# Reordering a two-lane decoder kernel: next sequence's FFN moved up, the convolution cut in three, one projection by tiles, two more buffers

## The chip, the cores and the metric

One Trainium2 chip, eight cores in two dies (cores 0 to 3 and 4 to 7). Each core computes two of the sixteen sequences, and no core waits for another. The metric is the device time in microseconds of the slowest core. The runs of this program show a fast state and a slow one: in the slow one the cores of one die (sometimes of both) record a lower granted TensorE clock, and the time is longer. For the kernel before, fast runs took from 6699 us and slow ones up to 7793. Wherever I compare kernels below, I use one of two things: the *fast runs* (no die over 1% longer than the other at a lower clock, and no run over 1.5% above the fastest of its kernel), or the *undisturbed dies*, by which I mean the dies of any run whose clock (the median of its four cores) is within 0.003 of the best of that kernel on that chip, each by its slowest core. The second gives more samples, because also in a slow run one die is usually undisturbed (of after's nine slow runs, in eight). It has no confidence interval here; I give its number of samples.

## The reference

A decoder of two layers, model width 1024, 2048 positions, FFN width 2816. Per layer:

```python
x = x + 0.5 * swiglu_ffn(rms_norm(x, ffn1_norm[l]), ffn1_w_up[l], ffn1_w_down[l])
h = rms_norm(x, mix_norm[l])                     # one projection h @ w_in, split over four groups
o_a = hgrn2_mixer(...)                           # gated recurrence, chunkwise
o_b = gla_mixer(...)                             # gated linear attention, chunkwise
o_c = dilated_attention_mixer(...)               # three dilated windows, partial rotary
o_d = conformer_conv_mixer(...)                  # GLU -> causal depthwise conv 31 -> LayerNorm -> swish
x = x + jnp.concatenate([o_a, o_b, o_c, o_d], axis=-1) @ w_out[l]
x = x + memory_cross_attention(rms_norm(x, cross_norm[l]), rms_norm(mem, mem_norm[l]), ...)
x = x + 0.5 * swiglu_ffn(rms_norm(x, ffn2_norm[l]), ffn2_w_up[l], ffn2_w_down[l])
# after the layers: rms_norm(x, final_norm)
```

The four groups o_a to o_d read the same `h` and are independent of each other until they are added into `x` through `w_out`. The change uses that freedom, and the freedom between two sequences.

## The kernel before

The kernel is written as a program that *records* operations. Every operation belongs to one of two lanes: **F** (the FFNs, with PSUM banks 0 to 3 and the weight buffers WBF and WS) and **M** (mixer and cross attention, with banks 4 to 7 and the sixteen buffers MU). A list scheduler then fixes the order on each engine: for each engine and lane it looks at the next 40 operations in program order, and takes the one that can start first by its own estimates. So the two lanes mix freely, but a lane can't look far beyond its own place in the program. All operations are issued from one line, which is why every profile line below reads L347, and why I go by tiles: HF, FB and WBF belong to the FFN, HM, MU, TPM and TBM to M, CF and CB are constants, X is the residual.

The program order, in halves `h` of 1024 positions (a tile `tt` is 512):

```python
self.load_x(0, 0)
for s in range(self.nseq):
    self.ffn(0, "ffn1", PV_FFN1, 0)
    if s == 0:
        self.load_x(0, 1); self.setup_tables()
    else:
        self.final(s - 1, 1); self.load_x(s, 1)          # lane M
    self.ffn(0, "ffn1", PV_FFN1, 1)
    for l in range(nd):
        for h in range(2):
            self.mixer(l, s, h)                          # lane M
            self.cross(l, h)                             # lane M
            if l == nd - 1 and h == 1:
                self.final(s, 0)                         # lane M
                if s + 1 < self.nseq: self.load_x(s + 1, 0)
            self.ffn(l, "ffn2", PV_FFN2, h)              # lane F
            if l + 1 < nd: self.ffn(l + 1, "ffn1", PV_FFN1, h)
self.final(self.nseq - 1, 1)
```

The mixer of one half, and the convolution with its two round trips through DRAM (tensors `ud` and `zd`), which re-lay the data:

```python
def mixer(self, l, s, h):
    ...
    self.rmsnorm(self.M, self.HM, "HM", ...)
    for cc in range(2): self.gla(l, h, "A", cc)
    self.w_out(l, h, 0, self._o)
    self.gla(l, h, "B", 0)
    self.w_out(l, h, 256, self._o)
    oc = [self.attn(l, s, h, cc) for cc in range(2)]
    self.w_out(l, h, 512, oc)
    self.conv(l, h)

def conv(self, l, h):
    for cc in range(2):                      # GLU of h, then written to ud
        ...
        self.dma(self.ud_d[...], u3, reads=[("MU", U)], writes=[("UD", h, cc)])
    self.dma(uc, self.ud_d[...], ...)        # and read back in another layout
    for b in range(4):                       # 16 x 5 matmuls with band matrices, statistics
        ...
    mean, var = ...                          # LayerNorm, swish -> z
    ...
    for cc in range(2):                      # z written to zd and read back
        self.dma(self.zd_d[...], z[...], ...)
        self.dma(self.mu(OD[cc]), self.zd_d[...], ...)
    self.out_proj("M", "w_out", l, 768, h, srcs, phased=True)
```

The FFN's down projection goes chunk by chunk of the output, each for both tiles: `for c0 ...: for dc ...: for t2 in range(2): ...`. `final` squares, scales and transposes two tiles and writes them out; the squares of any norm go through the small buffers TBF (lane F, two of them) or TBM (lane M, twelve).

The softmax here doesn't subtract the row's maximum and nothing guards it: scores larger than these inputs give would overflow.

Of the kernel before, what the change touches and what calls it, by code (L numbers as in the profile page):

```python
# [12 lines left out]
ALU = mybir.AluOpType  # L13

D = 1024
# [479 lines left out]
NTPF, NTBF = 3, 2  # L495
# [14 lines left out]
class Lane:  # L510
    def __init__(self, name, PS, TP, TB):
        self.name = name
        self.PS, self.TP, self.TB = PS, TP, TB
        self.psp = Pool("PS" + name, len(PS))
        self.tpp = Pool("TP" + name, TP.shape[1])
        self.tbp = Pool("TB" + name, TB.shape[1])

    def ps(self):
        i = self.psp.get()
        return i, self.PS[i], ("PS" + self.name, i)  # L520

    def tp(self):
        i = self.tpp.get()
        return i, self.TP[:, i, :], ("TP" + self.name, i)

    def tb(self):
        i = self.tbp.get()
        return i, self.TB[:, i, :], ("TB" + self.name, i)


class Builder:
# [23 lines left out]
    def slab(self, lane, name, l, c0, ncols, r0=0, nrows=D, swap=False):  # L555
        kc = nrows // 128
        n = kc * ncols
        assert n <= 1024
        if lane == "F":
            j = self.wbf.get()  # L560
            buf, key = self.WBF[:, j, :], ("WBF", j)
        else:
            j = self.mup.get()
            buf, key = self.mu(j), ("MU", j)
        wid = (name, l, c0, ncols, r0, swap)
        dst = buf[:, 0:n]
        if wid in self.wd_ids:
            i = self.wd_ids[wid]
            self.dma(dst, self.wd_d[i, :, 0:n], reads=[("WD", i)], writes=[key])
        else:  # L570
            i = len(self.wd_ids)
            assert i < NWD
            self.wd_ids[wid] = i
            if lane == "F":
                w = self.ws_rr
                self.ws_rr = (w + 1) % NWS
                ws, wsk = self.WS[:, w, 0:n], [("WS", w)]
            else:
                w = self.mup.get_run(2)
                ws, wsk = self.mu(w, 2).bitcast(F32)[:, 0:n], self.muk(w, 2)  # L580
            self.dma(ws.rearrange("p (k c) -> p k c", k=kc), self.wcols(name, l, c0, ncols, r0, nrows), writes=wsk)
            if swap:
                s5 = ws.rearrange("p (kh d) -> p kh d", d=64)
                d5 = dst.rearrange("p (kh d) -> p kh d", d=64)
                for a, b, c in ((0, 8, 8), (8, 0, 8), (16, 16, 48)):
                    self.E("pool", "tensor_copy", d5[:, :, a:a + c], s5[:, :, b:b + c], reads=wsk, writes=[key])
            else:
                self.E("pool", "tensor_copy", dst, ws, reads=wsk, writes=[key])
            if lane == "M":
                self.mup.free(w, 2)  # L590
            self.dma(self.wd_d[i, :, 0:n], dst, reads=[key], writes=[("WD", i)])
        return j, dst.rearrange("p (k c) -> p k c", k=kc), key
# [27 lines left out]
    def build(self):  # L620
# [23 lines left out]
        with ExitStack() as st:  # L644
# [24 lines left out]
            self.M = Lane("M", PS[4:8], TPM, TBM)  # L669
            self.wbf = Pool("WBF", NWBF)  # L670
# [31 lines left out]
    def program(self):  # L702
        self.em.lane = "M"
        self.setup_consts()
        nd = self.depth
        self.load_x(0, 0)
        for s in range(self.nseq):
            self.ffn(0, "ffn1", PV_FFN1, 0)
            if s == 0:
                self.load_x(0, 1)  # L710
                self.setup_tables()
            else:
                self.final(s - 1, 1)
                self.load_x(s, 1)
            self.ffn(0, "ffn1", PV_FFN1, 1)
            for l in range(nd):
                for h in range(2):
                    self.mixer(l, s, h)
                    self.cross(l, h)
                    if l == nd - 1 and h == 1:  # L720
                        self.final(s, 0)
                        if s + 1 < self.nseq:
                            self.load_x(s + 1, 0)
                    self.ffn(l, "ffn2", PV_FFN2, h)
                    if l + 1 < nd:
                        self.ffn(l + 1, "ffn1", PV_FFN1, h)
        self.final(self.nseq - 1, 1)
# [102 lines left out]
    def load_x(self, s, h):  # L830
        self.em.lane = "M"
        E, L = self.E, self.M
        ident = self.CF[:, CF_IDENT:CF_IDENT + 128]
        for tb in range(h * 8, h * 8 + 8):
            for hf in range(2):
# [7 lines left out]
                tt = tb // 4  # L843
# [33 lines left out]
    def out_proj(self, lane, wname, l, r0, h, srcs, scale=1.0, phased=False):  # L877
# [4 lines left out]
        for c0 in range(0, D, ncol):  # L882
            di, dw, dk = self.slab(lane, wname, l, c0, ncol, r0=r0, nrows=n * 128)
            for dc in range(c0 // 128, (c0 + ncol) // 128):
                co = dc * 128 - c0
                for t2 in range(2):
                    tt = 2 * h + t2
                    sl = slice(tt * TT, (tt + 1) * TT)
                    pa, psa, pka = L.ps()
                    for k in range(n):  # L890
                        rhs = srcs[k][0](t2)
                        E("pe", "matmul", psa[:, :], dw[:, k, co:co + 128], rhs, start=(k == 0), stop=(k == n - 1),
                          reads=[dk, srcs[k][1](t2)], writes=[pka], signal=(k == n - 1))
                    x, y = self.X[:, dc, sl], psa[:, :]
                    if phased:
                        x, y = x.rearrange("p (t f) -> p t f", f=8), y.rearrange("p (f t) -> p t f", f=8)
                    E("dve", "scalar_tensor_tensor", x, y, float(scale), x, ALU.mult, ALU.add,
                      reads=[pka, ("X", dc, tt)], writes=[("X", dc, tt)])
                    L.psp.free(pa)
            self.unslab(lane, di)  # L900

    def ffn(self, l, pre, pvcol, h):
# [4 lines left out]
        for (fa, fb) in ((0, 8), (8, 16), (16, 22)):  # L907
# [19 lines left out]
            self.out_proj("F", wdn, l, fa * 128, h, srcs, scale=0.5)  # L927
# [3 lines left out]
    def final(self, s, h):  # L931
        self.em.lane = "M"
        E, L = self.E, self.M
        identf = self.CF[:, CF_IDENT:CF_IDENT + 128]
        gcol = DP_FINAL
        for tt in (2 * h, 2 * h + 1):
            sl = slice(tt * TT, (tt + 1) * TT)
            ri, rap, rk = self.norm_stats(L, tt)
            for c in range(8):
                E("dve", "scalar_tensor_tensor", self.X[:, c, sl], self.X[:, c, sl], self.DP[:, gcol + c:gcol + c + 1], rap, ALU.mult, ALU.mult,  # L940
                  reads=[("X", c, tt), rk, "DP"], writes=[("X", c, tt)])
            L.tpp.free(ri)
            for q in range(4):
                tb = tt * 4 + q
                for hf in range(2):
                    pi, ps, pk = L.ps()
                    for c4 in range(4):
                        c = hf * 4 + c4
                        E("pe", "transpose", ps[:, c4 * 128:(c4 + 1) * 128], self.X[:, c, tb * 128:(tb + 1) * 128], identf,
                          reads=[("X", c, tt), "CF"], writes=[pk], signal=(c4 == 3))  # L950
                    oi, oap, ok = L.tp()
                    if hf == 0:
                        E("act", "activation", oap, ps[:, :], AF.Copy, reads=[pk], writes=[ok])
                    else:
                        E("dve", "tensor_copy", oap, ps[:, :], reads=[pk], writes=[ok])
                    L.psp.free(pi)
                    self.out_toks.append(self.dma(self.y_d[s, tb * 128:(tb + 1) * 128, hf * 512:(hf + 1) * 512], oap, reads=[ok]))
                    L.tpp.free(oi)

    def mixer(self, l, s, h):  # L960
# [3 lines left out]
        self.rmsnorm(self.M, self.HM, "HM", l * DP_L + PV_MIX, h)  # L964
        for cc in range(2):
            self.gla(l, h, "A", cc)
        self.w_out(l, h, 0, self._o)
        self.gla(l, h, "B", 0)
        self.w_out(l, h, 256, self._o)
        oc = [self.attn(l, s, h, cc) for cc in range(2)]  # L970
        self.w_out(l, h, 512, oc)
        self.conv(l, h)
# [364 lines left out]
    def conv(self, l, h):  # L1337
        E, L = self.E, self.M
        pb = l * PV_L
        CF, CB, PV = self.CF, self.CB, self.PV  # L1340
        H, hn = self.HM, "HM"
        phs = CB[:, CB_PHS:CB_PHS + 128]
# [24 lines left out]
        self.dma(uc, self.ud_d[:, T0:T0 + 132].rearrange("(g p) t -> p g t", p=128), reads=[("UD", hh, cc) for hh in range(h + 1) for cc in range(2)] + [("UDP", q) for q in range(16)], writes=uck)  # L1367
        Y = self.mup.get_run(4)
# [63 lines left out]
        self.mup.free(Z, 2)  # L1432
        srcs = [((lambda t2, u=u: self.mu(u).rearrange("p (f t) -> p f t", f=8)[:, :, t2 * 64:(t2 + 1) * 64]), (lambda t2, u=u: ("MU", u))) for u in OD]
# [168 lines left out]
```

## Time and profile before

| | |
|---|---|
| median of the first 7 runs | 7577 us (6699 to 7793) |
| median of all 18 runs | 7423 us |
| fast runs | 6699 to 6711 us |
| profiled run, die 0, die 1 | 6672 us, 6756 us |
| PE (TensorE) busy / idle on core 3, undisturbed die | 6141 / 540 us |
| matmuls | 38,720 |

The page is that of core 5, the slowest. The first lesson of this case is that core 5's die was disturbed, so here I show core 3, of the undisturbed die; times that I compare with the kernel after are its times. These are the page's busy shares of PE and its granted clock over 40 slices (in tenths; the page is core 5's):

```profile
PE   6999959999999999995999997799999999999689
...
PEclk7778979999999999998999998999999999999899
```

The digits below 8 in the first row, after the start (slices 6, 19, 25 and 26, 38), are where F has run dry. The 7s at the start of the second row are the part that I overlooked: there core 5 has a clock of about 0.8 while PE is busy. The windows view of both cores over that start (us, then busy us of PE, PEld, DVE, ACT and POOL, then granted clock, DMA share, GB/s), first core 5, then core 3:

```profile
400.00:700.00 300.00, 292.22 (x1716) 133.58 (x1717) 169.46 (x289) 120.74 (x211) 22.67 (x24) 0.81 0.35 99
```

```profile
0.00:400.00 400.00, 310.20 (x1552) 152.98 (x1553) 183.14 (x295) 148.86 (x255) 92.19 (x93) 0.91 0.80 221
400.00:700.00 300.00, 300.00 (x2254) 151.66 (x2253) 173.46 (x299) 121.74 (x215) 28.73 (x33) 1.00 0.45 126
775.00:999.00 224.00, 132.74 (x625) 58.42 (x624) 92.86 (x129) 79.63 (x140) 31.54 (x29) 0.82 0.39 116
2948.00:3155.00 207.00, 134.77 (x634) 60.86 (x632) 92.78 (x130) 80.74 (x143) 9.70 (x8) 0.84 0.20 58
4082.00:4293.00 211.00, 133.65 (x646) 59.58 (x645) 97.60 (x137) 84.51 (x149) 9.70 (x8) 0.84 0.23 66
6205.00:6415.00 210.00, 136.26 (x640) 59.97 (x638) 95.09 (x133) 81.02 (x143) 9.70 (x8) 0.85 0.20 57
```

With the same program, core 3 starts 2254 matmuls between 400 and 700 us and core 5 starts 1716, at a clock of 0.81 against 1.00. (The counts are not of the same matmuls, as core 5 is already behind by then.) The clock records in the trace of before hold three values: 1 and 0.5 on every core, and 0.8125 on the cores of die 1 alone. Neighbouring 128x512 matmuls of core 5 start 216 ns apart where the record holds 1, 263 ns at 0.8125 and 427 ns at 0.5 (medians of 21,041, 1740 and 369 pairs). The last four rows are the four M-only stretches: PE idle 91, 72, 77 and 74 us (length less PE busy).

### The profile page before, as it was taken

To read this page: it belongs to the slowest core of one execution; us is meant where nothing else is said; L and a number is where in the kernel's file an instruction comes from. 1 tells how busy PE (TensorE), PEld (TensorE's weight loads), DVE (VectorE), ACT (ScalarE), POOL (GpSimd) and SP (SyncE) were. 2 spreads that over 40 slices of the span, in tenths; PEclk is the share of its full clock that TensorE was granted. 3 is DMA by queue.
4 is the path that set the end of the run, shared out by engine and by line. 5 is a ranking of instruction groups with operands and counts; after the bars stand their busy time and mean duration, and the time that the engine had idled before them with its cause. 6 is when DMAs were issued, how large, how long until landed. Compare 5 with 4: busy or idle time off the path is not lost.

```text
span 6760.3 us, 111547 instructions; the slowest of 8 cores (6658.6 to 6760.3 us)
## 1 busy us (share of the span) xinstructions
PE 6232.5 (92%) x38720; PEld 3033.4 (45%) x38720; DVE 3505.3 (52%) x5620; ACT 2735.9 (40%) x4773; POOL 504.8 (7%) x495
## 2 busy tenths in 40 slices
PE   6999959999999999995999997799999999999689
PEld 3444524544445444452445454345454444445244
DVE  4255436555375646543453654554646555564444
ACT  3253234344343535333443533443435344443343
POOL 1300111112200101110000000000000000000000
PEclk7778979999999999998999998999999999999899
DMA  8933444556733443541343223122332223222222
GB/s 215 255 101 100 116 126 132 166 143 188 222 105 113 133 132 111 169 123 56 111 131 102 60 74 83 48 68 76 99 109 58 77 74 93 69 70 76 67 73 85
DMA packets 775235, 745.54 MB, mean 110 GB/s; under 512 B 121600, under 2 KB 555680, under 8 KB 774688
## 3 DMA queue, kind: packets, MB, share of 16 engines
q1 hardware_dynamic: 774688, 738.41, 38.1%
q8 instruction: 323, 5.29, 0.3%
q14 instruction: 224, 1.84, 0.1%
HBM read 590.31 MB, written 147.93 MB: 109 GB/s over the span
## 4 chain that ended last, share of the span: by engine, by line
PE 83%; DVE 5%; DMA 4%; SPq 3%; issue 2%; ACT 2%; POOL 0%; ACTq 0%; POOLq 0%; DVEq 0%
PE ps L347 83%; SPq L347 3%; DVE HM L347 2%; DVE HF L347 1%; DVE MU L347 1%; DMA ud<-MU 1%; ACT TPM L347 1%; ACT TBM L347 1%; DMA MU<-ud 1%; DVE X L347 0%; DMA zd<-MU 0%; POOL MU L347 0%; DVE TPM L347 0%; DMA MU<-cross_wo 0%; DMA MU<-zd 0%
## 5 line engine op out<-in xcount | busy, mean ns | idle before, releaser
L347 PE MATMUL ps<-HF,WBF 128*128 128x512 bf16 x11264 | 2633.1, 389 | 80.1 <-DVE HF L347 48.7
L347 PEld LDWEIGHTS ps<-HF,WBF 128*128 128x128 bf16 x11264 | 1096.3, 100 | 1408.0 <-issue 299.8
L347 DVE SCALAR_TENSOR_TENSOR X<-ps,X 128x512 f32<-128x512 f32 x1536 | 1018.3, 688 | 846.8 <-PE ps L347 843.9
L347 PE MATMUL ps<-FB,WBF 128*128 128x512 bf16 x5632 | 1320.1, 386 | 11.6 <-POOL WBF L347 8.4
L347 ACT ACTIVATE TPF<-ps 128x512 f32<-128x512 f32 x704 | 419.1, 595 | 1576.2 <-PE ps L347 1484.4
L347 PE MATMUL ps<-MU 128*128 128x512 bf16 (+7 forms) x5680 | 811.3, 313 | 229.2 <-DMA MU<-zd 114.3
L347 PE MATMUL ps<-HM,MU 128*128 128x512 bf16 (+1 forms) x3968 | 920.8, 386 | 54.3 <-DVE HM L347 34.2
L347 ACT ACTIVATE TPF<-TPF 128x512 f32<-128x512 f32 x1440 | 903.3, 629 | 98.9 <-ACT TPF L347 2.2
L347 DVE TENSOR_TENSOR FB<-ps,TPF 128x512 bf16<-128x512 f32 x704 | 485.6, 690 | 806.2 <-PE ps L347 801.9
L347 PEld LDWEIGHTS ps<-FB,WBF 128*128 128x128 bf16 x5632 | 545.2, 99 | 677.7 <-issue 105.9
L347 PEld LDWEIGHTS ps<-MU 128*128 128x128 bf16 (+4 forms) x5680 | 424.8, 121 | 616.2 <-issue 374.8
L347 DVE TENSOR_TENSOR TPF<-ps,TPF 128x512 f32<-128x512 f32 x704 | 481.4, 684 | 387.7 <-ACT TPF L347 358.8
L347 ACT ACTIVATE TBM<-ps 128x512 bf16<-128x512 f32 (+6 forms) x656 | 360.2, 580 | 708.1 <-PE ps L347 707.0
L347 PEld LDWEIGHTS ps<-HM,MU 128*128 128x128 bf16 (+1 forms) x3968 | 388.0, 99 | 540.9 <-issue 121.4
L347 DVE TENSOR_TENSOR MU<-ps,TPM 128x512 bf16<-128x512 f32 x256 | 226.3, 905 | 338.7 <-ACT TPM L347 279.4
L347 POOL CAST WBF<-WS 128x1024 bf16<-128x1024 f32 (+1 forms) x272 | 280.1, 1032 | 1296.6 <-PE ps L347 1040.9
L347 ACT ACTIVATE TPM<-TPM 128x512 f32<-128x512 f32 (+1 forms) x548 | 334.2, 619 | 49.1 <-DVE TPM L347 25.2
L347 POOL TENSOR_TENSOR MU<-MU,PV 128x512 f32<-128x512 f32 x64 | 76.2, 1221 | 3387.6 <-DVE MU L347 3387.6
L347 PE MATMUL ps<-TBM,CB 128*64 128x128 bf16 (+7 forms) x2768 | 278.9, 259 | 48.2 <-ACT TBM L347 47.9
L347 ACT ACTIVATE MU<-ps 128x512 bf16<-128x512 f32 (+1 forms) x176 | 105.0, 597 | 510.1 <-PE ps L347 508.0
L347 ACT ACTIVATE TBM<-X 128x512 bf16<-128x512 f32 x320 | 192.2, 625 | 263.0 <-DVE X L347 228.9
L347 ACT ACTIVATE TPM<-ps 128x512 f32<-128x512 f32 x256 | 151.4, 592 | 362.8 <-PE ps L347 356.2
(74 smaller groups left out, 3223.0 us busy)
## 6 DMA issues: line engine op xcount, KB each, us to landing
WBF<-wd SPq DMA_DIRECT2D x720, 256.0 KB, 2.6
WS<-ffn_w_up SPq DMA_DIRECT2D x176, 512.0 KB, 6.0
MU<-wd SPq DMA_DIRECT2D x344, 256.0 KB, 3.0
wd<-WBF SPq DMA_DIRECT2D x240, 256.0 KB, 4.0
wd<-MU SPq DMA_DIRECT2D x136, 256.0 KB, 3.7
WS<-ffn_w_down SPq DMA_DIRECT2D x64, 512.0 KB, 5.0
MU<-w_in SPq DMA_DIRECT2D x56, 512.0 KB, 5.5
MU<-wcd SPq DMA_DIRECT2D x128, 160.0 KB, 2.9
```

The costliest lines, as they stand in the source:

```text
L347: ins = getattr(e, fn[0])(*fn[1], **fn[2])
```

## The change

Its intent is to give PE other work while one chain waits. (a) The next sequence's ffn1 goes beside the last mixer step of this one, with `final` and the load of x tile by tile in lane F, in halves of WS; so F no longer runs dry between the sequences. (b) The convolution is cut at its two round trips, and other work of the mixer is put between. (c) The very last chunk of the last down projection goes tile by tile, so that the final norm of the first tile can run beside the second's matmuls. (d) TBF gets four buffers instead of two. The core of the diff:

```diff
-NTPF, NTBF = 3, 2
+NTPF, NTBF = 3, 4
...
+            self.FX = Lane("F", PS[0:4], self.WS.rearrange(...), TBF, base=self.F, tpname="WS")
...
-                    if l == nd - 1 and h == 1:
-                        self.final(s, 0)
-                        if s + 1 < self.nseq:
-                            self.load_x(s + 1, 0)
-                    self.ffn(l, "ffn2", PV_FFN2, h)
+                    self.ffn(l, "ffn2", PV_FFN2, h, tm=(l + 1 == nd and h == 1 and s + 1 == ns))
                     if l + 1 < nd:
                         self.ffn(l + 1, "ffn1", PV_FFN1, h)
-        self.final(self.nseq - 1, 1)
+                        continue
+                    for tt in (2 * h, 2 * h + 1):
+                        self.final(s, tt, "M" if h == 1 and s + 1 == ns else "F")
+                        if s + 1 < ns:
+                            self.load_x("F", self.FX, s + 1, tt)
+                    if s + 1 < ns:
+                        self.ffn(0, "ffn1", PV_FFN1, h)
...
+        for t_outer in ((0,), (1,)) if tile_major else ((0, 1),):
+            for c0 in range(0, D, ncol):
...
+            self.out_proj("F", wdn, l, fa * 128, h, srcs, scale=0.5, tile_major=(tm and fb == 22))
...
+        uc = self.conv_in(l, h)
         for cc in range(2):
             self.gla(l, h, "A", cc)
         self.w_out(l, h, 0, self._o)
+        od = self.conv_mid(l, h, uc)
         self.gla(l, h, "B", 0)
         self.w_out(l, h, 256, self._o)
+        self.conv_out(l, h, od)
         oc = [self.attn(l, s, h, cc) for cc in range(2)]
         self.w_out(l, h, 512, oc)
-        self.conv(l, h)
```

## The prediction

> **What bounds the kernel now.** I read the cores first, then the busy shares, then TensorE's waits, then TensorE stretch by stretch, and last the instructions in the worst gap.
>
> Cores and dies (span, mean granted clock):
>
> ```profile
> die 0 (median of its cores): 6671.6 us, clock 0.963
> die 1 (median of its cores): 6756.0 us, clock 0.949
> ```
>
> The profiled execution (6760 us) is close to the fast state: die 1 is 1.3% longer. But the seven times are 6699, 6711, 6762 and then 7577, 7581, 7786, 7793: three fast, four in the slow state. The quoted median of 7577 is a slow run; everything that a profile can tell me is about fast ones, some 6705 us. I keep the two apart.
>
> The page, busy share of the span by engine, and the waits in which TensorE (PE) stood still (us in total, times, longest):
>
> ```profile
> PE 6232.5 (92%) x38720; PEld 3033.4 (45%) x38720; DVE 3505.3 (52%) x5620; ACT 2735.9 (40%) x4773; POOL 504.8 (7%) x495
> ...
> PE ps L347 <- DMA MU<-zd: 114.3, 5, 30.3
> PE ps L347 <- DMA MU<-ud: 71.1, 8, 15.2
> PE ps L347 <- ACT TBF L347: 48.9, 80, 1.2
> PE ps L347 <- DVE HF L347: 48.7, 21, 4.1
> PE ps L347 <- ACT TBM L347: 47.9, 41, 1.8
> PE ps L347 <- DVE HM L347: 34.2, 14, 6.7
> PE ps L347 <- DMA TPM<-x: 28.6, 8, 8.7
> ```
>
> PE is the bound; every other engine is at half or less. The change keeps the number of matmuls (38,720 in both builds), so all it can win is in the 6760 - 6232 = 528 us in which PE is idle. The two largest waits are for zd and ud, the DRAM round trips of the convolution (185 us).
>
> Where the 528 us lie, as busy time in eight stretches (us, PE, PEld, DVE, ACT, POOL, clock, DMA):
>
> ```profile
> 0.00:400.00 400.00, 335.59 (x1432) 157.36 (x1432) 158.24 (x254) 132.17 (x223) 90.72 (x93) 0.79 0.81 221
> 845.00:1080.00 235.00, 141.37 (x660) 61.23 (x658) 101.48 (x141) 85.83 (x151) 32.22 (x30) 0.83 0.39 116
> 3037.00:3242.00 205.00, 124.97 (x616) 57.99 (x616) 95.53 (x139) 80.19 (x142) 9.70 (x8) 0.85 0.21 62
> 3242.00:3780.00 538.00, 521.36 (x2622) 256.72 (x2623) 248.31 (x384) 230.37 (x394) 0.00 (x0) 0.98 0.37 108
> 4168.00:4370.00 202.00, 123.55 (x601) 54.88 (x600) 93.18 (x135) 79.97 (x142) 9.70 (x8) 0.83 0.22 63
> 6290.00:6510.00 220.00, 139.32 (x678) 63.93 (x677) 103.97 (x147) 88.03 (x155) 9.70 (x8) 0.86 0.21 61
> 6510.00:6735.00 225.00, 225.00 (x1042) 102.34 (x1041) 90.42 (x136) 86.04 (x144) 0.00 (x0) 0.99 0.28 78
> 6735.00:6760.00 25.00, 13.11 (x78) 10.19 (x75) 17.08 (x26) 7.71 (x14) 0.00 (x0) 0.83 0.45 168
> ```
>
> Idle PE time in the order of the rows: 64 (start-up), 94, 80, 17, 78, 81, 0, 12. The rows with 94, 80, 78 and 81, together 333 us, are the case. In each the FFN lane (F) has run dry, and the mixer lane (M) alone can't fill PE. All else, 528 - 333 - 64 - 12 - 17 = 102, is spread as 5 to 20 us at every stage boundary. One FFN half is 1056 matmuls, at 215 ns each 227 us; a mixer-plus-cross step is 2263/8 = 283 us of PE. Most M steps run beside two FFN halves (454 us) and PE stays full. Those four run beside one: step (layer 0, half 0) and step (layer 1, half 1) of each sequence, as ffn1 of the next sequence waits in program order behind them.
>
> What M alone looks like (start, duration, instruction, idle before it and what ended it), the last M-only stretch, the convolution and the begin of the cross attention:
>
> ```profile
> 6302.95 1.89 PE L347 MATMUL ps<-HM,MU 128*128 128x512 bf16 x8 [0.20 <-DVE MU L347]
> 6320.00 5.49 PE L347 MATMUL ps<-MU 128*128 128x128 bf16 x55 [15.16 <-DMA MU<-ud]
> ...
> 6358.93 9.87 PE L347 MATMUL ps<-MU 128*128 128x512 bf16 x32 [27.85 <-DMA MU<-zd]
> 6368.80 3.70 PE L347 MATMUL ps<-TBM,CB 128*128 128x512 bf16 x16
> 6379.24 8.81 PE L347 MATMUL ps<-HM,MU 128*128 128x512 bf16 x32 [6.74 <-DVE HM L347]
> ```
>
> 15.2 + 27.9 and about 5 in small pieces: the convolution costs 48 us of the 81, the norm and the cross attention the other 33.
>
> [...]the trace agrees (465 matmuls in 100 us of a dense stretch, 215 ns). [...]The trace agrees: clock 0.83 to 0.86 in the four gappy rows, 0.98 and 0.99 in the dense ones; so closing gaps also speeds the matmuls next to them. [...]The ud write takes 7.1 us to land and the read 4.7, by the page's table of issues; today M has nothing to do in between.
>
> **The change, part by part.** I take the counts of each stretch from the order of PE instructions in the two builds, priced at 215 ns per 512 columns[...].
>
> *a. Next sequence's ffn1 moved beside the last M step, final and load moved to the F lane.* The M-only stretches at 3037 and 4168 hold 113.7 and 114.4 us of PE work before. In the changed order the stretches without FFN matmuls there hold 49.1 and 40.1 us, and they also contain final and load (CF,X and CF,WS transposes, 64 each): they last because F itself now waits. F's chain there: per tile, 8 squares of 0.62 us, rstd 1.3, 8 scalings of 0.69 (5.4 in all), 8 evictions at about 0.65 on two engines, an output DMA (2.4) before its half of WS is free, a load (5.1), 8 evictions again; the second tile overlaps the first. I estimate 60 us a time, against 40 to 49 us of PE work: idle 15 to 20 each, 35 together. Before, 3020 to 4370 cost 80 + 17 + 78 = 175. After: 35 plus ordinary stage boundaries (9 us at 3760, same kind as before; two of them) 18, so 53. Saved: about 120.
>
> *b. Convolution cut in three, before, between and after the recurrences.* It gives nothing where F fills the gaps, save the 2 to 4 us pieces at 1500, 2300, 4800 and 5560 (about 10). In the two M-only stretches that stay (845 and 6290) the order of work is now attention then cross. The first grows from 111 to 148 us of PE work, with both attention units in it; the last is 107 against 115.5, with one. An attention unit alone would repeat every 2 us (scores to first exp 0.74, two exps 1.09, then the two score banks are free), with 1.3 us of PE work: 0.7 us idle, 12 units per channel pair, 8 us; two pairs about 17, and the value round trip 5. So first: 33 + 17 + 5 = 55 against 94, saved 39; last: 33 + 8 + 4 = 45 against 81, saved 36.
>
> *c. Final norm tile by tile at the end.* The end row (25 us, 12 idle) has two tiles' scalings of 5.4 us each one after the other on DVE. With the last projection tile by tile the first tile's scaling and output lie beside the second's matmuls: saved 6 to 8. It costs 8 more slab loads (192 KB, 2.3 us to land) at a DMA share of 0.28: hidden.
>
> *d. TBF 2 to 4 buffers.* The 48.9 us waiting for TBF are 0.6 us each: the pace of ACT's squares, which buffers don't change. Run-ahead while the last projection chunks come in may give 5 to 8 us.
>
> Sum: 120 + 10 + 39 + 36 + 7 + 6 = 218 us. Fast runs: 6705 - 218 = about 6490, ratio 0.968.
>
> **Rivals.** *F's chain blocks the queue.* PE takes its instructions in a fixed order. If x lands later than the scheduler thought, a transpose waiting for it holds up M's matmuls behind it. Each load is 5.1 us to landing; 16 blocks of 2 us would make 30 us more per boundary: gain 155, 6550. Against it: load at 3242 to 3280 ran between FFN matmuls with 2 us idle. *Attention alone is worse than convolution alone.* If a unit takes 3.5 us instead of 2, the two stretches keep 40 more: 6530. For it: the first stretch has more left than before. *The clock takes the gain.* [...]The granted clock in dense late stretches is 0.98 to 1.0, which speaks against it in fast runs[...]. *Everything overlaps better than I think*: half the boundary idle goes too, 6420.
>
> **Range and chances.** Fast 6490, with 6420 to 6570 for 8 in 10; 2% is reached at 6571, a gain of 134 of my 218, so 0.82 for faster. Two of the rivals together would be needed for "same": 0.16. Slower needs a regression that no view hints at: 0.02. The quoted time is a median over both states. With the mix of before (four of seven slow) it falls in the slow one: 7577 less about the same microseconds, 7360; if more runs are fast, about 6490. The range must hold both, 6430 to 7640; the point stays with the state of the quoted median.
>
> **What would show it.** Right: no stretch without FFN matmuls between the sequences longer than some 70 us; PE's waits for zd and ud under 40 us together; idle PE time near 310 of 6490; PE busy time unchanged near 6230. Step a is wrong if PE waits for x or y transfers there by more than 40 us; b if the first M-only stretch is longer than 215 us; c if the end row still lasts 25. The whole is wrong if PE's busy time grows as idle falls.

The us of PE work counted under (a) and (b) were estimates; in the trace of before (core 3) matmuls of 512 columns start 216 ns apart and those of 128 columns on 128 rows 56 ns. The "fixed order" of PE is seen in the traces: in before and in after, the six cores with complete records start their 38,720 matmuls in one and the same order; and at 2887.33 us of after (the timeline further below) M's matmuls come behind a transpose that waited 2.25 us for x. The remark that closing gaps speeds the matmuls beside them was borne out at 10.0 against 8.7 us for 32 of them (before_warm3).

## The result and the profile after

The quoted median, over seven runs, was 6893 us (6426 to 7496); that of before, now over 18 runs, was 7423. The ratio of the fast runs is 0.959, with a 95% interval of 0.957 to 0.961. (A ratio here is the mean time of one kernel's fast runs over that of the other's in the same rounds, so not quite the ratio of the medians quoted.) The three fast runs took 6426, 6431 and 6435 us. Results are correct.

So the change is faster, as predicted, and the range 6430 to 7640 held the median, but the point of 7360 was 467 us too high. Fast against fast, the prediction of 6490 was about 60 us too high: 0.968 predicted, 0.959 measured.

The page of after is of a fast run, slowest core 4. Its head, the busy line, the two rows by slices, and the medians of the dies:

```profile
span 6424.5 us, 111530 instructions; the slowest of 8 cores (6396.9 to 6424.5 us)
...
PE 6101.1 (95%) x38720; PEld 3007.7 (47%) x38720; DVE 3489.1 (54%) x5620; ACT 2720.3 (42%) x4773; POOL 509.1 (8%) x495
...
PE   6899979999899999999999989999999999999889
...
PEclk8999989999999999999999999999999999999999
```

```profile
die 0 (median of its cores): 6408.3 us, clock 0.979
die 1 (median of its cores): 6414.5 us, clock 0.978
```

Both dies are undisturbed, of the five low digits in PE's row one 7 is left (in the first M-only stretch), and the clock is higher (0.979 against 0.963 on die 0 of before). The waits of PE (us in total, times, longest), first core 3 of before, its two largest; then core 4 of after, its largest and two that the prediction named:

```profile
PE ps L347 <- DMA MU<-zd: 115.7, 5, 31.0
PE ps L347 <- DMA MU<-ud: 66.1, 8, 13.8
```

```profile
PE ps L347 <- POOL WBF L347: 35.0, 15, 6.3
PE ps L347 <- ACT TBM L347: 34.9, 37, 1.8
PE ps L347 <- DVE MU L347: 32.1, 20, 4.2
PE ps L347 <- DMA TPM<-x: 32.1, 10, 9.2
...
PE ps L347 <- ACT TBF L347: 12.6, 26, 1.1
PE ps L347 <- DMA WS<-x: 11.5, 9, 2.3
```

The waits for zd and ud, 182 us, no longer stand in the list at all. The rest is many small waits, none above 35 us in total. The windows of after (core 4) that answer to those of before; columns as before:

```profile
0.00:402.00 402.00, 312.85 (x1497) 153.11 (x1498) 175.07 (x275) 145.60 (x252) 92.23 (x94) 0.90 0.84 225
...
760.00:987.00 227.00, 174.35 (x1207) 87.64 (x1206) 107.53 (x163) 91.77 (x162) 24.09 (x25) 0.89 0.36 105
2872.00:2956.00 84.00, 69.12 (x780) 48.71 (x778) 44.64 (x77) 39.13 (x72) 0.00 (x0) 0.94 0.44 137
...
3708.00:3784.00 76.00, 58.43 (x505) 36.99 (x504) 51.31 (x85) 41.18 (x75) 0.00 (x0) 0.89 0.45 144
5998.00:6171.00 173.00, 131.63 (x855) 65.02 (x853) 83.87 (x136) 72.63 (x128) 0.00 (x0) 0.89 0.18 58
6405.00:6425.00 20.00, 10.63 (x52) 8.36 (x50) 10.70 (x17) 5.34 (x9) 0.00 (x0) 0.72 0.49 181
```

The two M-only stretches at the sequence boundary, 207 and 211 us long, have shrunk to 84 and 76 us. The first stretch is about as long as before (227 against 224 us), but has 1207 matmuls in it instead of 625. A few lines of the timeline in the stretch at 2872 show how work from both lanes now lies side by side (start, duration, instruction; in brackets the idle time before it and what ended it):

```profile
2887.33 0.63 PE L347 MATMUL ps<-CF,WS 128*128 128x128 f32 x4 [2.25 <-DMA WS<-x]
2887.89 0.56 PE L347 MATMUL ps<-MU 64*128 64x128 bf16 x8
...
2900.63 7.07 PE L347 MATMUL ps<-HM,MU 128*128 128x512 bf16 x32
...
2935.34 1.09 PE L347 MATMUL ps<-CF,WS 128*128 128x128 f32 x4 [1.51 <-DMA WS<-x]
```

CF,WS are the transposes of the newly loaded x, in lane F; MU and HM,MU are attention and projections, in lane M. The longest gap there is 2.3 us.

Idle time of PE by stretch, from the windows of the two undisturbed cores (length less PE busy; the F phases between are taken together):

| stretch | idle before (core 3) | idle after (core 4) | saved | predicted |
|---|---|---|---|---|
| start to the first M-only stretch | 90 | 97 | -7 | 0 |
| first M-only stretch | 91 | 53 | 38 | 39 |
| sequence boundary (2948 to 4293; 2872 to 4099) | 171 | 46 | 125 | 120 |
| last M-only stretch | 74 | 41 | 33 | 36 |
| end | 12 | 9 | 3 | 7 |
| all else, where F and M are both full | 102 | 78 | 24 | 16 |
| whole span | 540 | 323 | 216 | 218 |

The idle time fell by what was predicted, nearly row by row. But the span fell by 256 us between these two cores (6680.5 to 6424.5). The other 40 us are PE *busy* time: 6141 to 6101. The prediction said that it would not change. Where it fell is shown by the groups of PE instructions by form (count, busy us, mean ns of one, then idle before them and its releasers); before, core 3:

```profile
L347 PE MATMUL ps<-HF,WBF 128*128 128x512 bf16 x11264 | 2578.4, 383 | 86.7 <-DVE HF L347 46.0 <-DVE FB L347 23.0 <-POOL WBF L347 13.4
...
L347 PE MATMUL ps<-MU 128*128 128x512 bf16 x2304 | 565.8, 390 | 153.4 <-DMA MU<-zd 115.7 <-DVE MU L347 15.0 <-ACT MU L347 13.6
...
L347 PE MATMUL ps<-MU 128*128 128x128 bf16 x1152 | 85.6, 239 | 70.7 <-DMA MU<-ud 66.1 <-POOL MU L347 3.6 <-DMA MU<-wcd 0.7
```

and after, core 4:

```profile
L347 PE MATMUL ps<-HF,WBF 128*128 128x512 bf16 x11264 | 2576.1, 383 | 78.1 <-POOL WBF L347 27.1 <-DVE HF L347 26.5 <-DVE FB L347 19.2
...
L347 PE MATMUL ps<-MU 128*128 128x512 bf16 x2304 | 553.6, 384 | 31.7 <-DVE MU L347 13.5 <-POOL MU L347 10.2 <-ACT MU L347 6.9
...
L347 PE MATMUL ps<-MU 128*128 128x128 bf16 x1152 | 74.0, 220 | 6.7 <-DMA MU<-wcd 6.3
```

The big FFN group, two fifths of PE's time, hasn't changed (2578 to 2576). The two MU groups that came right behind the waits for zd and ud each lost 12 us, and the mean of the second fell from 239 to 220 ns with the same count. The norms' ones-matmuls together (from CB with TBM or TBF, 768 of them, not shown) lost another 18: 252 to 234 us. These three groups make up 42 us, which is the whole fall, with 2 us gained elsewhere. The clock records of the two cores agree in direction: time with the record 0.5 (half clock, or a cold clock, as I call it below) fell from 496 to 284 us. But only part of that time had PE busy (255 and 214 us). As neighbouring 128x512 matmuls start 427 ns apart there instead of 216, I estimate that half clock accounts for half of the 41, some 20 us. The rest of the 40 I can't place to the microsecond.

### The profile page after: what moved, and what is told of

Same layout as the page of the kernel before. It is cut to its first block, busy times and chain, and to the rows that moved or that the text cites. A ratio compares the mean times of both kernels' runs of the same rounds, so it can differ in the third digit from the quotient of the medians.

```text
span 6424.5 us, 111530 instructions; the slowest of 8 cores (6396.9 to 6424.5 us)
## 1 busy us (share of the span) xinstructions
PE 6101.1 (95%) x38720; PEld 3007.7 (47%) x38720; DVE 3489.1 (54%) x5620; ACT 2720.3 (42%) x4773; POOL 509.1 (8%) x495
## 4 chain that ended last, share of the span: by engine, by line
PE 83%; DVE 5%; SPq 4%; DMA 3%; issue 3%; ACT 2%; POOL 0%; DVEq 0%; ACTq 0%; POOLq 0%
PE ps L347 83%; SPq L347 4%; DVE HF L347 2%; DVE HM L347 2%; DVE MU L347 1%; ACT TBM L347 1%; DMA MU<-wcd 1%; ACT TPM L347 0%; DVE X L347 0%; DMA MU<-w_in 0%; DMA WS<-x 0%; DMA WS<-ffn_w_up 0%; DMA TPM<-x 0%; ACT TBF L347 0%; ACT TPF L347 0%
## 5 line engine op out<-in xcount | busy, mean ns | idle before, releaser
L347 PE MATMUL ps<-HF,WBF 128*128 128x512 bf16 x11264 | 2576.1, 383 | 78.1 <-POOL WBF L347 27.1
L347 PE MATMUL ps<-FB,WBF 128*128 128x512 bf16 x5632 | 1296.2, 380 | 9.6 <-POOL WBF L347 7.9
L347 PEld LDWEIGHTS ps<-FB,WBF 128*128 128x128 bf16 x5632 | 541.0, 98 | 652.0 <-issue 26.4
L347 PE MATMUL ps<-MU 128*128 128x512 bf16 (+7 forms) x5680 | 780.1, 305 | 62.0 <-DVE MU L347 21.5
L347 PEld LDWEIGHTS ps<-MU 128*128 128x128 bf16 (+4 forms) x5680 | 409.6, 118 | 422.6 <-issue 152.2
L347 ACT ACTIVATE TPM<-ps 128x512 f32<-128x512 f32 x232 | 137.3, 592 | 444.3 <-PE ps L347 442.9
L347 POOL CAST MU<-MU 128x1024 bf16<-128x1024 f32 (+2 forms) x154 | 148.7, 969 | 1159.9 <-PE ps L347 476.3
```

The source lines that it names most:

```text
L347: ins = getattr(e, fn[0])(*fn[1], **fn[2])
```

## The experiments

The theory: what is won is idle time in the four stretches where F was dry, by (a) at the boundary and by (b) in all four; (c) and (d) give little; and the matmuls behind closed gaps run faster. The rivals: that one of (a) and (b) does nearly all; that the cold clock is a cause of its own, so that keeping PE busy with useless matmuls would win time without closing any gap; and, for what remains, that a different order could still be better. In some of the expectations below, theory A is that a gap costs its own length only, and theory B that it also costs by the matmuls beside it, at half clock. For B, core 3 of before has the record 0.5 for 273 us of the four M-only stretches; PE is busy in 102 of them, so I estimate the loss at half of that, 51 us. Times in the table are means of undisturbed dies, and ratios are of fast runs with their 95% interval.

| kernel | chip | undisturbed dies, us (samples) | before on that chip | ratio to before |
|---|---|---|---|---|
| conv_only | 12 | 6498 (8) | 6670 (10) | 0.973 [0.971, 0.976] |
| order_only | 12 | 6558 (6) | 6670 | 0.983 [0.980, 0.985] |
| before_warm | 12 | 6697 (6) | 6670 | none, one fast run |
| after_tb2 | 12 | 6410 (7) | 6670 | none, one fast run |
| before_warm2 | 14 | 6782 (10) | 6672 (7) | 1.008 [1.003, 1.014] |
| after_again | 14 | 6408 (6) | 6672 | 0.956 [0.951, 0.962] |
| after_no_tm | 14 | 6407 (10) | 6672 | 0.953 [0.949, 0.958] |
| after_ct_late | 14 | 6408 (6) | 6672 | 0.955 [0.949, 0.962] |
| before_warm3 | 7 | 6691 (8) | 6694 (10) | 0.999 [0.993, 1.004] |
| after_again2 | 7 | 6417 (5) | 6694 | 0.963 [0.957, 0.969] |
| after_xlane | 7 | 6407 (7) | 6694 | 0.959 [0.949, 0.968] |

All eleven runs gave correct results. On chip 14 the fast runs of before reach from 6676 to 6769 us, so several are slightly disturbed; there the ratios of fast runs lie away from the ratio of undisturbed dies (before_warm2: 6782 over 6672 is 1.016, and 1.008 by fast runs). I rely on the undisturbed dies for differences below a per cent, and call nothing below 10 us a difference.

**conv_only**: the kernel before with (b) alone.

```diff
+        uc = self.conv_in(l, h)
         ... gla A, w_out ...
+        od = self.conv_mid(l, h, uc)
         ... gla B, w_out ...
+        self.conv_out(l, h, od)
         ... attn, w_out ...
-        self.conv(l, h)
```

> The kernel before with the convolution cut in three and nothing else. Both theories price the idle time of TensorE alike: four stretches without FFN matmuls stay, each loses the ud and zd waits (some 45 us) and gets attention gaps (8 to 17 us) instead, so 36 us each, and 10 us elsewhere: idle time 155 us less, from about 540 to 385. Theory A (only idle time counts): ratio to before 1 - 155/6705 = 0.977. Theory B [...]: the cold clock beside the M-only stretches was no smaller in the changed kernel (15 to 19 us and 12 to 13 us), so this part brings at most 10 us more: 0.975 to 0.977. Waits for ud and zd together under 40 us.

Measured: 172 us less than before. On core 5 (undisturbed) the waits for zd and ud no longer appear, and the largest wait of PE is now of another kind:

```profile
PE ps L347 <- ACT TBM L347: 59.3, 64, 1.8
PE ps L347 <- DVE MU L347: 47.1, 26, 2.5
```

PE idle is 373 us against 540, a fall of 167 where 155 were expected, and PE busy is 6123 against 6141. The four M-only stretches are still there, at 218, 165, 171 and 167 us (224, 207, 210 and 210 before). So the convolution's waits are worth nearly their face value (182 us of waits, 172 of time) as long as all four stretches are dry: the pieces of the mixer that were put between do fill them. Part (b) alone is the larger half of the change.

**order_only**: the change with (a) alone: two TBF buffers, no tile order, the convolution in one piece as before.

```diff
-NTPF, NTBF = 3, 4
+NTPF, NTBF = 3, 2
...
-            self.out_proj("F", ..., tile_major=(tm and fb == 22))
+            self.out_proj("F", ..., tile_major=False)
... and mixer() and conv() as in the kernel before
```

> The kernel before with only the next sequence's ffn1, final and load moved to the FFN lane; convolution in one piece, 2 buffers in TBF, no tile-major end. Idle time in the stretch from the last step of sequence 0 to the first of sequence 1 falls from 170 to 50 if F's chain is some 60 us and the convolution is covered there (gain 120, ratio 0.982), to 90 or more if the convolution's waits fall into F's chain (gain 80 or less, ratio 0.988). Theory B adds about 15 us of clock, as the changed kernel has 16 us of cold-clock loss there against 31: 0.980.

Measured: 112 us less. The waits for zd and ud on core 3:

```profile
PE ps L347 <- DMA MU<-zd: 62.3, 3, 29.5
...
PE ps L347 <- DMA MU<-ud: 48.1, 7, 14.2
```

110 of the 182 us are left: 86 us in the first and last stretch, which keep their 217 and 220 us, and 24 us in small waits elsewhere, while the two stretches at the boundary shrink to 85 and 89 us. This tells the parts apart: (a) closes two of the four holes by filling them with F, (b) closes the waits in all four. They overlap in two, which is why 172 + 112 = 284 is more than the 260 of the two together on this chip (after_tb2, next).

**after_tb2**: the change with (d) undone.

```diff
-NTPF, NTBF = 3, 4
+NTPF, NTBF = 3, 2
```

> The changed kernel with 2 buffers in TBF again. Predicted worth of the buffers 5 to 8 us: 6431 to 6438, waits for TBF back from 12.6 to some 40 us. If they are worth nothing, the waits return but the time stays within 2 us, since the squares set the pace.

Measured: 6410 us, against 6408 of the change itself on chip 14 and 6417 on chip 7. The change itself did not run on this chip, 12, but before took 6670 us here and 6672 on chip 14. (d) is worth nothing that I can see. Yet its wait did come back: on core 5 of this kernel

```profile
PE ps L347 <- ACT TBF L347: 31.2, 54, 0.9
PE ps L347 <- ACT TBM L347: 28.2, 31, 2.3
...
PE ps L347 <- DVE MU L347: 24.4, 19, 2.5
...
PE ps L347 <- DVE HM L347: 21.1, 14, 6.7
```

and on core 5 of the change run again (after_again; its die was undisturbed, and both cores have a span of 6398 us)

```profile
PE ps L347 <- ACT TBM L347: 35.8, 40, 1.8
PE ps L347 <- DVE MU L347: 32.2, 20, 4.2
...
PE ps L347 <- DVE HM L347: 28.7, 16, 6.7
...
PE ps L347 <- ACT TBF L347: 11.6, 25, 1.1
```

The four buffers take 20 us from the waits for TBF, and those for TBM, MU and HM rise by 23 together. PE idle is 295 and 297 us. A wait removed from one lane became small waits of the other: the sum, not the line, is what counts.

**after_again, after_again2**: the change itself, unedited, as the reference of its two chips.

> The changed kernel itself, beside the others of this call on the same chip: ratio to before 0.959 as on record, 6395 to 6430 on undisturbed dies. It is the yardstick for the next two.

> The changed kernel beside the other two on the same chip: ratio to before 0.956 to 0.960; undisturbed dies 6395 to 6435.

Measured: 6408 us on chip 14 and 6417 on chip 7, 264 and 278 us less than before there. The gain repeats on each chip. The profiled executions of both fell in the slow state: the cores of die 0 had a mean clock of 0.868 and 0.869 in one and 0.899 to 0.901 in the other, those of die 1 0.977 to 0.981. If 0.8125 in place of 1 makes the difference, as in the records of before, I estimate from these means some 4,200 and 2,900 us of it.

**after_no_tm**: the change with (c) undone.

```diff
-            self.out_proj("F", ..., tile_major=(tm and fb == 22))
+            self.out_proj("F", ..., tile_major=False)
```

> The changed kernel with the last down projection chunk by chunk for both tiles, as before. Predicted worth of the tile order 6 to 8 us: undisturbed dies 6 to 8 us above the changed kernel, time from the last FFN matmul to the end 21 to 23 us instead of 15 to 16. If the reloaded slabs cost what the overlap wins, no difference.

Measured: 6407 us against 6408. From the end of the last FFN matmul to the last computing instruction it now takes 22.2 us (core 3) instead of 15.4 (after_again, core 5), so (c) does shorten the tail as intended; but without it the last FFN matmul itself comes as much earlier (at 6373.0 us instead of 6379.4). The tile order costs 8 more weight loads, and PE's waits for WBF are 24.6 us with it (after_again, core 5) and 19.9 without (core 3). But over the undisturbed cores the two ranges overlap (20.4 to 26.4, and 18.7 to 23.5), so what the price is stays open; that (c) is worth nothing in total is shown.

**before_warm, before_warm2, before_warm3**: the kernel before, with useless matmuls put where PE is idle, to see whether the cold clock goes. If the cold clock behind the gaps costs time of its own, some of it should come back though the gaps stay. The results are correct, as the extra matmuls go to a bank of lane F that nobody reads.

```diff
+    def warm(self, n, keys):
+        for _ in range(n):
+            pi, ps, pk = L.ps()                      # a PSUM bank of lane F
+            for k in range(2):
+                E("pe", "matmul", ps[:, :], ones, self.CB[:, 0:TT], ..., reads=["CB"] + keys, ...)
+            L.psp.free(pi)
... before_warm: 120 pairs after ffn1(0, half 1) and after the last layer's ffn2(half 0), no keys
... before_warm2: in conv(), in the four dry steps
+            if cc == 1 and l == h: self.warm(30, [("MU", U)])     # the ud wait
+        if l == h: self.warm(56, [mk])                            # the zd wait, before the last Exp of var
... before_warm3: only this, behind the Exp
+        if l == h: self.warm(58, [mk])
```

> The kernel before with 240 useless matmuls (constants, into a PSUM bank of the FFN lane that nobody reads) behind each FFN half that leaves the lane dry; in the order of instructions they lie mostly in the convolution's waits. Results stay right. Theory A (a gap costs its own length only): no gain, 0 to 20 us slower, ratio 1.000 to 1.003. Theory B (the matmuls beside a gap run at half clock): of the 51 us that cold clock costs in the four M-only stretches, what lies beside the convolution, some 5 us each, comes back: 20 us, ratio 0.997, and the loss by cold clock in these stretches is 6 to 8 us each instead of 12 to 15.

> A better placed filler in the kernel before: in the four steps with an M-only stretch, 60 useless matmuls that may start when the last GLU product is there (the ud wait) and 112 that may start when the mean is there (the zd wait), so that they lie in these waits and nowhere else: 172 x 215 ns = 37 us each time, of some 43 us idle. Theory A (a gap costs its own length only): undisturbed dies stay at the some 6670 us of before on this chip, or a few us above. Theory B (a gap also makes the matmuls beside it run at half clock): in the first filler run the first M-only stretch was 10 us shorter and its cold-clock loss 7 instead of 15 us, so 6 to 10 us in each of four stretches: 24 to 40 us faster, 6630 to 6646, ratio 0.994 to 0.996.

> The filler once more, with the mistake of the last one mended: there the useless matmuls read the tile of the mean before its last activation wrote it, so the chain itself waited 24 us for them. Now 116 of them are issued after that activation, in the zd wait of the four M-only steps, 25 us of the 28 to 31 us gap, and nothing waits for them. Theory B (matmuls beside a gap run at half clock): the 32 output-projection matmuls behind the gap take 6.9 us instead of 10.0, and the squares' sums behind them 3.5 instead of 3.7; four times 3 us, 12 us less on undisturbed dies. Theory A: the 32 matmuls still take 10 us, or the gap is longer by what they gain; no change in the time.

*before_warm* missed its aim: the scheduler put part of the fillers into the F phases, where PE was busy (one phase took 424 us instead of 386, and the dry stretch behind it 170 instead of 207), and the kernel got 26 us slower. Too much moved at once, so it says nothing about the clock.

*before_warm2* got 110 us slower, by a mistake of mine that is instructive. The fillers read the tile with the mean and variance, and the Exp that finishes the variance writes that tile; so the Exp had to wait until all fillers had read. In the timeline of core 3:

```profile
816.30 24.33 PE L347 MATMUL ps<-CB 128*128 128x512 bf16 x112 [1.83 <-ACT TPM L347]
868.10 10.15 PE L347 MATMUL ps<-MU 128*128 128x512 bf16 x32 [27.46 <-DMA MU<-zd]
```

The fillers take 24.3 us, and the whole chain to zd then starts: PE waits another 27.5 us. In the four steps the fillers of the zd wait take 24 to 27 us each, 102 together, which is most of the 110. It shows that in these stretches the convolution's chain sets the time one to one, which is what (b) lives on.

*before_warm3* repaired that. In the kernel before (core 3) and here (core 4), the projection behind the zd wait:

```profile
851.94 10.02 PE L347 MATMUL ps<-MU 128*128 128x512 bf16 x32 [30.96 <-DMA MU<-zd]
```

```profile
815.00 26.19 PE L347 MATMUL ps<-CB 128*128 128x512 bf16 x113 [2.61 <-ACT TPM L347]
841.03 8.71 PE L347 MATMUL ps<-MU 128*128 128x512 bf16 x32
```

The fillers fill the wait to its end, and the 32 matmuls behind it take 8.7 us instead of 10.0. (In one of the four steps 0.8 us of the wait is left.) In before, core 3 has the record 0.5 from 821.8 to 856.0 us, over the first 4 us of those 10. So the cold clock is real, at 1.3 us a time (1.7 in the last step, where before took 10.4), less than half of the 3.1 that were expected; in four steps that makes some 6 us. The kernel took 6691 against 6694 us: 3 us, which is noise. The rival is not borne out as a cause of its own at any size that matters: a cold clock costs a little time behind each gap (1.3 to 1.7 us here), and the change wins that too as it removes gaps. The ud waits were not filled in a run that tests this.

**after_ct_late**: the change, with the setting up of the convolution's matrices put after the first cross_kv. In the trace of the change, VectorE stands at 74 us for 11 us for the first of these matrices to load and then works on them for 10 us, and PE waits 19 us for it.

```diff
-        self.conv_matrices()                         # end of setup_tables()
...
             self.cross_kv(l, s)
+            if l == 0 and s == 0:
+                self.conv_matrices()
```

> A try at a better version: the changed kernel with the banded convolution matrices built after the first cross-attention keys and values instead of at the start, where VectorE waited 11.4 us for the taps' transfer and then took 10.4 us for 14 products while FFN evictions stood behind them in its queue and TensorE waited 18.9 us. If nothing takes the place of that wait, 15 to 19 us faster than the changed kernel, ratio to before 0.956 to 0.957. Rival: the start is bound by the float32 weights (220 GB/s over the first 400 us), and the wait moves to the next slab: under 5 us.

Measured: 6408 against 6408. The wait at the start moved: the first M-only stretch became 234 us long instead of 227, and a stretch of 28 us without FFN matmuls appeared at 1337. What bounds the first 402 us, with 89 us of PE idle at a DMA rate of 225 GB/s (in the trace of the change), stays open.

**after_xlane**: after_no_tm, with every second head of the cross attention in the two remaining dry steps given to lane F, so that they use F's idle banks, weight buffers and its place in the queue.

```diff
-                    self.cross(l, h)
+                    self.cross(l, h, dry=((s, l, h) in ((0, 0, 0), (ns - 1, nd - 1, 1))))
...
             for hh in range(2):
+                ln = "F" if dry and hh == 1 else "M"
+                self.em.lane = ln
+                L = self.F if ln == "F" else self.M
...
-                    w = self.slab("M", "cross_wq", l, (hd * 2 + dc) * 128, 128)
+                    w = self.slab(ln, "cross_wq", l, (hd * 2 + dc) * 128, 128)
```

> A try at a better version: the changed kernel (last projection chunk by chunk, which cost nothing), with the odd heads of the cross attention put on the FFN lane's queue, PSUM banks and slabs in the two steps that still have an M-only stretch. Alone, a head leaves TensorE idle 0.8 to 2.9 us at each of its exps and its norm, some 25 us in each of the two stretches. If two heads interleave, half of that goes: 10 to 15 us in each stretch, 20 to 30 in all, ratio to before 0.953 to 0.956 where the changed kernel has 0.958. If ScalarE is what both heads wait for (each head 16 activations of 0.6 us), or the added PE waits sit in the queue in front of the other head, no gain.

Measured: the two stretches fell to 211 and 151 us on core 5 (227 and 172 on core 5 of after_again2), but the time is 6407 us, 10 us below after_again2, which is at the edge of what I call a difference, and the intervals of the ratios overlap. It is nominally the fastest version on its chip, but no proven improvement over the change. It also says something about the rest: 36 us taken from the M-only stretches brought at most 10 us of time. Perhaps the work taken out has to be done in the F phases; that was not followed up.

## Why the prediction was right or wrong

**Direction, size of the idle time, and its places: right.** 218 us of idle were predicted to go, and 216 went; the three big rows of the table agree within 5 us. The criteria that bear on this held: the waits for zd and ud (set under 40 us) are 0, waits for x at the boundary are 11.5 us (set under 40), PE is idle for 323 us (predicted about 310). Putting other work between the issue of these transfers and the wait for them turned 182 us of waits into none.

**(a), 120 us: right**, at 125. The no-FFN stretches of 84 and 76 us are a little longer than the "some 70" and their idle of 15 and 18 us is what was estimated (15 to 20). The rival in which F's chain blocks the queue would have shown as waits of 30 us per boundary; it didn't come.

**(b), 39 and 36 us: right**, at 38 and 33. The criterion "wrong if the first M-only stretch is longer than 215 us" was badly chosen: the stretch lasts 227 us, but with twice the matmuls in it, because M work moved into it out of the F phase before, which got shorter (384 us before, 358 after). A length by itself doesn't tell what is idle.

**(c) 7 us and (d) 6 us: wrong by their whole size.** Undone one at a time, both give 0. For (c) the tail was shortened, from 22.2 to 15.4 us behind the last FFN matmul, but that matmul came later. For (d) the prediction said "the pace of ACT's squares, which buffers don't change", and the wait for TBF did fall by 20 us; as much reappeared as waits of the other lane. The step that failed is the same in both: adding a local saving to the sum, without asking what takes its place. That the idle sum still fits within 2 us is partly luck: the balanced stages saved 24 us where 10 + 6 were predicted, and the start lost 7.

**"PE busy time unchanged near 6230": wrong.** This is the term of the sum that was mis-sized: the sum priced idle time alone, and the fast gain came out as 218 us where the two traces show 256 and the undisturbed dies of the later chips 260 to 278. Two errors lie in it. The 6230 was that of a disturbed core; on the undisturbed die it was 6141. And it fell by 40 us more, to 6101, in the groups behind the gaps. The prediction had this in hand ("closing gaps also speeds the matmuls next to them") and left it out of its sum.

**The state: wrong, and the largest miss in the quoted number.** The step reads "the point stays with the state of the quoted median". It took the slow state for one level, 7577, and moved it down by 217, to 7360; the median came out at 6893. The range held it, but a range that spans both states says little. For after's slow runs lie anywhere from 6547 to 7496 us, and within the same run the other die (its slowest core) in all but one stays between 6416 and 6439. The mean clock of a die goes with it: 0.955 in the run of 6547 us, 0.89 to 0.92 in those of 6767 to 6934, 0.80 in that of 7496. In the trace of before the cores with a lower mean are those with records of 0.8125, and they have them for only a part of the span. For the slow executions profiled later I estimate, from the mean clocks of their two dies, some 2,900 us of it (conv_only, after_again2: 0.90 against 0.975 and 0.979) and 4,200 us (after_again: 0.868 against 0.979). So a median over such runs falls between levels; by this estimate it depends on how long the low clock lasted. The step before it failed too: it held that no trace shows the low clock. The trace of before does: the cores of its die 1 have 0.8125 for 408 to 545 us, cores 4 and 5 near their start (105 to 674 us), cores 6 and 7 at their end (6319 to 6756 us). It could have been read there, from the 7s in the clock row of core 5 and from the other die beside it. Core 6 of before (columns as in the windows above):

```profile
105.00:674.00 569.00, 525.99 (x3336) 259.40 (x3394) 299.05 (x492) 226.90 (x398) 104.26 (x105) 0.97 0.61 176
6319.00:6756.00 437.00, 401.35 (x1529) 174.59 (x1557) 166.77 (x250) 151.24 (x256) 0.00 (x0) 0.80 0.21 62
```

The 84 us between the two dies, which I called "close to the fast state", are about that clock: core 5 had PE busy for 530 us at 0.8125 instead of 1, which by my estimate (530 x 0.1875) loses 99 us. In the fast run of after no core has a record of 0.8125, with PE busy for 94 or 95% of the span on all eight. Why a die goes to the low clock in one run and not in the next, and for how long, is open; no run here was made to test it.

**Small slips in its working.** In the rivals, 36 attention units at 1.5 us more make 54 us, not 40, and half of the 102 us of boundary idle takes 6490 to about 6440, not 6420. The prices of short matmuls were not read from the trace. In that of before, core 3, matmuls of 128 columns on 128 rows start 56 ns apart, and smaller ones can follow much closer: of 960 pairs of the form 64*64 64x64, 60% start 5 ns or less apart.

## What to carry to other kernels

When an engine is the bound and idles in a few stretches, price the idle by stretch, and ask of each part which stretch it fills; savings that lie in the same stretch can't be added, and a small wait removed in a full stage can come back as another (here 20 us of waits for TBF became 23 of others). Add the busy time behind each gap to the account, but expect it to be small: here some 40 us beside 216. Before reading the slowest core's profile, compare its die with the other: if its clock is lower in any part, read a core of the better die, and quote no single "slow" level.
